# Two-block transformer kernel on one core: first attention's scores from float32r pairs, and two of the recurrence's four products per level on VectorE

## The chip, the cores and the metric

The kernel runs on one core of one Trainium2 chip. The metric is device time in microseconds (us) of one execution; lower is better. The engines are named as the profile names them: PE (TensorE matmul), PEld (TensorE weight load), DVE (VectorE), ACT (ScalarE), POOL (GpSimd), SP (the queue that issues most transfers).

## What is computed

Two transformer blocks, one behind the other, on 256 tokens (272 with 16 meta tokens in the first block) of width 2048, all in float32. What matters for this change is the first attention's scores and the gated recurrence of the second block:

```python
# differential attention, 8 heads, head size 128, queries in blocks of 128 (and the 16 meta tokens)
s1 = einsum('bhqd,bhkd->bhqk', q1, k1) * scale
s2 = einsum('bhqd,bhkd->bhqk', q2, k2) * scale
a = softmax(mask(s1)) - lam * softmax(mask(s2))

# gated recurrence, 8 heads of 128, over the tokens t
f_t = lb + (1 - lb) * sigmoid(z_t);   k_t = (1 - lb) * sigmoid(-z_t)
state_t = f_t * state_{t-1} + k_t v_t;   o_t = q_t state_t
```

## The kernel before, in words

**Weights.** All weight matrices come through one stream of 6240 tiles of 128x128, in the order in which PE uses them. `Weights.take` (lines 113 to 132) hands out a tile. A *slot* is 8 tiles. When PE's program reaches slot s, ACT is given the rounding of slot s+3 to float32r (`high`, line 84, from `raw` into `hi`), and DVE the remainder of slot s+2 (`low`, line 93, into `lo`), so that three float32r matmuls (x high by w high, x low by w high, x high by w low) stand for one of float32. `hi` has 4 buffers and `lo` has 3, so the writes for slots s+3 and s+2 go into the buffers that slot s-1 gives up.

**Ticks.** After that, once per slot, `take` calls `step_bg` (line 173). It moves the first generator of the queue `bgq` one step on, and then the first of `bgq2`; a step is what lies between two `yield`s. Heads of the first attention (`attend`) and of the second (`slide`) are in `bgq`, behind the set-up generators `first_parameters` and `rotary_tables`; the groups of the recurrence (`hgrn`) are in `bgq2`. Twice per slot `step_evac` moves the generators on that take projections out of PSUM. Every engine runs its instructions in the order in which they are written; this order is what the `yield`s set, and nothing reorders it.

**First attention, `attend` (line 785).** Its first step is empty. The second transposes v on PE (lines 792, 793) and splits it into float32r parts (`parts`, lines 766 on ACT and 767 on DVE). The third computes the scores in plain float32, six matmuls per head (lines 800 to 802): for each of the two components 144, 272 and 16 columns against 128, 128 and 16 rows. Each float32 matmul is two records of the trace. Then DVE adds the mask and takes the maxima (lines 808 to 814). q and k reach the tile `qk` from `qkv_evac`, which turns them on POOL (lines 888 to 890).

**Second attention, `slide` (line 1103).** One step has the scores (PE lines 1112, 1113) and the mask and maxima on DVE (1118 to 1125); the next has the exponentials on ACT (1128 to 1131) and, behind them, three small DVE instructions (1132 to 1134) that wait for them.

**Recurrence, `hgrn` (line 1223).** Four groups of two heads. A group works through eight levels, m = 1, 2, 4 ... 128. Per level, `products` (line 1242) issues on POOL qp (1245) and kp (1246), the operands of the level's matmuls, and for m < 128 two in-place updates, x by f (1251) and f by f (1252), for the next level. Tick lv issues `products(lv + 1)`, then the matmuls of level lv on PE (1266; 1274 for the last), then a predicated copy on DVE (1268). So the operands of level lv+1 are issued one tick before PE wants them. Groups 0 to 2 run beside the projections of the next group and one `slide` each; group 3 runs beside `gates` (1314). `hgrn_evac` (line 1188) takes the gate out of PSUM: sum, scale by the norm on DVE (1212), tanh on ACT (1214), and from it f and k by two scalings on POOL (1215, 1216).

Of the kernel before, what the change touches and what calls it, by code (L numbers as in the profile page):

```python
# [135 lines left out]
def tile_two_block_model(ctx, tc, w, xT, pT, cv_d, cs_d, msk_d, pos_d, gains, spill, aside, out):  # L136
# [27 lines left out]
    def att_t():  # L164
        return att_p.tile([P, 512], F32, tag="att", name="att")
# [224 lines left out]
    def split_pair(hi, lo, src):  # L390
        act(hi.bitcast(F32R), src)
        yield
        V.tensor_tensor(lo.bitcast(F32R), src, hi, ALU.subtract)
# [271 lines left out]
    with tc.tile_pool(name="ph0", bufs=1) as ph:  # L665
# [3 lines left out]
        for i in range(8):  # L669
            nc.sync.dma_start(h[:, 2 * i:2 * i + 2, :], xT[:, 2 * i:2 * i + 2, :])  # L670
            if i % 2 == 0 and i // 2 < RAW:
                W.load(i // 2)
        mskf = ph.tile([P, 7, 64], F32, tag="mskf", name="mskf")
        pt = ph.tile([P, 2, S], F32, tag="pt", name="pt")
        pi_t = ph.tile([P, S], I32, tag="pos", name="pos")
        x0 = Normed(h, 0, L, "pre0", tmp)
        neg_lam, sub, gnorm = prm[:, 0:1], prm[:, 1:3], prm[:, 3:4]
        fB, fA, kB, kN = prm[:, 8:16], prm[:, 16:24], prm[:, 24:32], prm[:, 32:40]
# [83 lines left out]
        def parts(n, tag, src, meta=None):  # L762

            hi, lo = meta or (ph.tile([P, n], F32, tag=tag + t, name=tag + t) for t in "hl")
            rows = NM if meta else P
            act(hi[:rows].bitcast(F32R), src)
            V.tensor_tensor(lo[:rows].bitcast(F32R), src, hi[:rows], ALU.subtract)
            return hi.bitcast(F32R), lo.bitcast(F32R)
# [16 lines left out]
        def attend(hd):  # L785
            st = heads[hd]
            qk, vf = st["qk"], st["v"]
            yield
            tv, tm = att_t(), att_t()
            for d in range(2):  # L790
                for k in range(2):
                    PE.transpose(tv[:, k * 256 + d * P:k * 256 + (d + 1) * P], vf[d][:, NM + k * P:NM + (k + 1) * P], ident)
                PE.transpose(tm[:NM, d * P:(d + 1) * P], vf[d][:, :NM], ident)
            vt, vm = parts(512, "vt", tv), parts(256, "vm", tm[:NM, :256], meta_v)
            yield
            sa, sb = att_t(), [att_t(), att_t()]
            sav = sa[:, :288].rearrange("p (c k) -> p c k", c=2)
            scv = sa[:NM, 288:320].rearrange("p (c k) -> p c k", c=2)
            for c in range(2):
                PE.matmul(sav[:, c], qk[:, c, NM:NM + P], qk[:, 2 + c, :144], start=True, stop=True)  # L800
                PE.matmul(sb[c][:, :L], qk[:, c, NM + P:], qk[:, 2 + c, :], start=True, stop=True)
                PE.matmul(scv[:, c], qk[:, c, :NM], qk[:, 2 + c, :NM], start=True, stop=True)
            ea = ph.tile([P, 2, 144], F32, tag="ea", name="ea")
            eb = ph.tile([P, 2, L], F32, tag="eb", name="eb")
            em = meta_e[:NM, :2 * NM].rearrange("p (c k) -> p c k", c=2)
# [240 lines left out]
    with tc.tile_pool(name="ph2", bufs=1) as ph:  # L1046
# [141 lines left out]
        def hgrn_evac(nt, acc):  # L1188
            kind, hd = (nt - 12) // 8, (nt - 12) % 8
            gr, i = hd // 2, hd % 2  # L1190
            st = hg.setdefault(gr, {})

            def slot(tag, bufs=1):
                if tag not in st:
                    st[tag] = hp.tile([P, 2, S], F32, tag="hg_" + tag, name=tag, bufs=bufs)
                return st[tag][:, i]

            if kind in (0, 3):
                t = tmp()
                yield from total(acc, t)  # L1200
                V.tensor_tensor(t, t, R2[0], ALU.mult)
                o = slot("q" if kind == 0 else "g")
                yield
                act(o, t, AF.Tanh, scale=0.5)
                yield
                V.scalar_tensor_tensor(o, o, 1.0, t, ALU.add, ALU.mult)
                if kind == 3 and i == 1:
                    bgq2.append(hgrn(gr))
            elif kind == 1:
                t = tmp()  # L1210
                yield from total(acc, t)
                V.tensor_tensor(t, t, R2[0], ALU.mult)
                yield
                act(t, t, AF.Tanh, scale=0.5)
                G.tensor_scalar(slot("f", 2), t, fB[:, hd:hd + 1], fA[:, hd:hd + 1], ALU.mult, ALU.add)
                G.tensor_scalar(slot("k", 2), t, kN[:, hd:hd + 1], kB[:, hd:hd + 1], ALU.mult, ALU.add)

        QP = [hp.tile([P, S], F32, tag=f"qp{i}", name=f"qp{i}") for i in range(2)]
        KP = [hp.tile([P, 2, S], F32, tag=f"kp{i}", name=f"kp{i}") for i in range(2)]
# [3 lines left out]
        def hgrn(gr):  # L1223
            st = hg[gr]
            q, k, f, vt, g = (st[n] for n in "qkfvg")
            x = mid().rearrange("p (i n) -> p i n", i=2)
            G.memset(x, 1.0)
            st_ = mid().rearrange("p (a b) -> p a b", a=4)
            s01 = mid()[:, :256].rearrange("p (a b) -> p a b", a=2)
            dg = att_t()  # L1230
            for i in range(2):
                for b in range(2):
                    c = slice(b * P, (b + 1) * P)
                    PE.matmul(dg[:, (2 * i + b) * P:(2 * i + b + 1) * P], k[:, i, c], q[:, i, c], start=True, stop=True)
            V.tensor_tensor(st_, dg.rearrange("p (a b) -> p a b", a=4), ident.unsqueeze(1).to_broadcast([P, 4, P]), ALU.mult)
            yield

            def halves(t, m):
                u = t.rearrange("p i (s e m) -> p (i s) e m", e=2, m=m)
                return u[:, :, 0, :], u[:, :, 1, :]  # L1240

            def products(lv):
                m = 1 << lv
                qp, kp = QP[lv % 2], KP[lv % 2]
                G.tensor_tensor(qp.rearrange("p (q m) -> p q m", m=m), halves(q, m)[1], halves(f, m)[1], ALU.mult)  # L1245
                G.tensor_tensor(halves(kp, m)[0], halves(k, m)[0], halves(x, m)[0], ALU.mult)  # L1246
                if m < P:
                    f0, f1 = halves(f, m)
                    x0_, _ = halves(x, m)
                    n = S // m  # L1250
                    G.tensor_tensor(x0_, x0_, f1[:, :, m - 1:m].to_broadcast([P, n, m]), ALU.mult)  # L1251
                    G.tensor_tensor(f1, f1, f0[:, :, m - 1:m].to_broadcast([P, n, m]), ALU.mult)

            products(0)
            yield
            for lv in range(8):
                if lv < 7:
                    products(lv + 1)
                qp, kp = QP[lv % 2], KP[lv % 2]
                ps = att_t()  # L1260
                if lv < 7:
                    for i in range(2):
                        for b in range(2):
                            c = slice(b * P, (b + 1) * P)
                            t = slice((2 * i + b) * 64, (2 * i + b + 1) * 64)
                            PE.matmul(ps[:, t], kp[:, i, c], qp[:, t], start=True, stop=True)
                    m = 1 << lv
                    V.copy_predicated(
                        st_.rearrange("p a (s e m) -> p (a s) e m", e=2, m=m)[:, :, 1, :],
                        msk[:, lv].rearrange("p a (s m) -> p (a s) m", m=m),  # L1270
                        ps[:, :S].rearrange("p (q m) -> p q m", m=m))
                else:
                    for i in range(2):
                        PE.matmul(ps[:, i * P:(i + 1) * P], kp[:, i, :P], qp[:, i * P:(i + 1) * P], start=True, stop=True)
                    act(s01.rearrange("p a b -> p (a b)"), ps[:, :256])
                yield
            o = att_t()
            for i in range(2):
                PE.matmul(o[:, 2 * i * P:(2 * i + 1) * P], st_[:, 2 * i], vt[:, i, 0], start=True, stop=True)
                PE.matmul(o[:, (2 * i + 1) * P:(2 * i + 2) * P], s01[:, i], vt[:, i, 0], start=True, stop=False)  # L1280
                PE.matmul(o[:, (2 * i + 1) * P:(2 * i + 2) * P], st_[:, 2 * i + 1], vt[:, i, 1], start=False, stop=True)
            sq = tiny(4, "hsq")
            for a in range(4):
                junk = tmp()
                act(junk[:, :P], o[:, a * P:(a + 1) * P], AF.Square, accum_out=sq[:, a:a + 1])
            r = rows_rsqrt(sq, 4, scale=1.0 / P)
            yield
            os_ = mid().rearrange("p (a b) -> p a b", a=4)
            V.tensor_tensor(os_, o.rearrange("p (a b) -> p a b", a=4), r.unsqueeze(2).to_broadcast([P, 4, P]), ALU.mult)
            yield  # L1290
            ot = att_t()
            for a in range(4):
                PE.transpose(ot[:, a * P:(a + 1) * P], os_[:, a], ident)
            y = mid().rearrange("p (i n) -> p i n", i=2)
            V.scalar_tensor_tensor(y, ot.rearrange("p (i n) -> p i n", i=2), gnorm, g, ALU.mult, ALU.mult)
            yield from split_pair(yh[:, 2 * gr:2 * gr + 2, 0], yh[:, 2 * gr:2 * gr + 2, 1], y)
            yield
# [281 lines left out]
```

## Time and profile before

| | |
|---|---|
| median of 3 runs | 2394.36 us (2394.22 to 2395.17) |
| the profiled execution: its own time | 2394.97 us |
| its span | 2393.2 us |
| granted clock of PE, mean | 0.997 |
| busy share of the span | PE 99%, PEld 88%, DVE 61%, ACT 49%, POOL 23% |
| chain that ended last, by engine | PE 69%, POOL 3%, DVE 1%, DMA 1% |

The profiled execution's own time is 1.8 us more than its span (what lies around the first and last instruction) and 0.6 us more than the median. A busy PE isn't PE at its peak: matmuls are pipelined and their recorded durations overlap, so the cost of one is read from the distance of its start to the start of the next. Where a line stands for several instructions ("x8"), the first number is the start of the first and the second the time to the end of the last.

### The profile page before, as it was taken

To read this page: it belongs to the slowest core of one execution; us is meant where nothing else is said; L and a number is where in the kernel's file an instruction comes from. 1 tells how busy PE (TensorE), PEld (TensorE's weight loads), DVE (VectorE), ACT (ScalarE), POOL (GpSimd) and SP (SyncE) were. 2 spreads that over 40 slices of the span, in tenths; PEclk is the share of its full clock that TensorE was granted. 3 is DMA by queue.
4 is the path that set the end of the run, shared out by engine and by line. 5 is a ranking of instruction groups with operands and counts; after the bars stand their busy time and mean duration, and the time that the engine had idled before them with its cause. 6 is when DMAs were issued, how large, how long until landed. Compare 5 with 4: busy or idle time off the path is not lost.

```text
span 2393.2 us, 36724 instructions
## 1 busy us (share of the span) xinstructions
PE 2364.7 (99%) x14560; PEld 2112.0 (88%) x14560; DVE 1468.7 (61%) x2202; ACT 1162.5 (49%) x1931; POOL 545.0 (23%) x603
## 2 busy tenths in 40 slices
PE   8999999999999999999999999999999999999998
PEld 8999999998999888898888888888888888888876
DVE  7665555547767476667656566575545555556575
ACT  5444444545555464444444454564444444344463
POOL 5433222226322003455440121011100110011000
PEclk9999999999999999999999999999999999999999
DMA  6344444544555554334345556455555555555653
GB/s 253 142 152 154 157 156 158 196 177 172 190 193 216 206 218 158 144 141 155 145 159 193 184 187 246 176 193 187 214 205 186 187 193 189 186 188 193 255 196 138
DMA packets 64875, 439.08 MB, mean 183 GB/s; under 512 B 7104, under 2 KB 10304, under 8 KB 13760
## 3 DMA queue, kind: packets, MB, share of 16 engines
q1 hardware_dynamic: 59184, 413.81, 47.5%
q0 software_dynamic: 1904, 15.34, 1.6%
q10 hardware_dynamic: 3616, 7.59, 0.9%
q8 instruction: 114, 1.87, 0.3%
q14 instruction: 57, 0.47, 0.1%
HBM read 426.75 MB, written 9.96 MB: 182 GB/s over the span
## 4 chain that ended last, share of the span: by engine, by line
PE 69%; POOL 3%; DVE 1%; DMA 1%; issue 1%; ACT 0%; DVEq 0%; ACTq 0%; POOLq 0%; SPq 0%
PE acc L215 26%; PE acc L214 13%; PE acc L247 7%; PE acc L245 7%; PE acc L246 7%; PE acc L1092 2%; PE acc L217 1%; PE acc L211 1%; PE acc L210 1%; PE acc L209 1%; DMA raw<-w 1%; POOL b L1251 1%; PE att L215 1%; POOL qp L1245 1%; POOL kp L1246 0%
## 5 line engine op out<-in xcount | busy, mean ns | idle before, releaser
L93 DVE TENSOR_TENSOR lo<-raw,hi 128x1024 fp32r<-128x1024 f32 (+1 forms) x803 | 988.5, 1235 | 635.9 <-PE acc L247 183.8
L84 ACT CAST hi<-raw 128x1024 fp32r<-128x1024 f32 x780 | 814.7, 1047 | 616.2 <-PE acc L246 208.3
L215 PE MATMUL acc<-x,hi 128*128 128x512 f32 x2656 | 929.5, 395 | 1.1 <-DVE c L274 0.6
L214 PE MATMUL acc<-x,lo 128*128 128x256 f32 x2490 | 701.4, 282 | 0.4 <-DVE lo L93 0.3
L215 PEld LDWEIGHTS acc<-x,hi 128*128 128x128 f32 x2656 | 491.7, 188 | 102.4 <-DVE x L542 1.4
L214 PEld LDWEIGHTS acc<-x,lo 128*128 128x128 f32 x2490 | 470.0, 189 | 7.6 <-DVE lo L93 0.8
L209 PE MATMUL acc<-x,hi 128*128 128x272 f32 (+3 forms) x1232 | 358.9, 291 | 7.3 <-ACT hi L84 7.2
L211 PE MATMUL acc<-x,lo 128*128 128x272 f32 (+3 forms) x1232 | 355.8, 289 | 0.5 <-DVE lo L93 0.4
L210 PE MATMUL acc<-x,hi 128*128 128x272 f32 (+3 forms) x1232 | 355.2, 288 | 0.8 <-DVE x L426 0.8
L209 PEld LDWEIGHTS acc<-x,hi 128*128 128x128 f32 x1232 | 232.8, 189 | 8.4 <-ACT hi L84 7.2
L210 PEld LDWEIGHTS acc<-x,hi 128*128 128x128 f32 x1232 | 234.7, 191 | 2.0 <-DVE x L426 1.3
L211 PEld LDWEIGHTS acc<-x,lo 128*128 128x128 f32 x1232 | 232.5, 189 | 1.0 <-DVE lo L93 1.0
L168 ACT ACTIVATE c<-acc 128x256 f32<-128x256 f32 x210 | 80.1, 384 | 257.0 <-PE acc L215 254.8
L1381 POOL TENSOR_TENSOR c<-c,R 128x256 f32<-128x256 f32 x88 | 66.7, 759 | 579.0 <-DVE c L274 576.9
L247 PE MATMUL acc<-lo,up 128*128 128x512 f32 x352 | 138.7, 394 | 0.3 <-DVE lo L93 0.3
L245 PE MATMUL acc<-hi,up 128*128 128x512 f32 x352 | 138.8, 394 | 0.0
L246 PE MATMUL acc<-hi,up 128*128 128x512 f32 x352 | 138.4, 393 | 0.0
L274 DVE TENSOR_TENSOR c<-c,acc 128x256 f32<-128x256 f32 x206 | 84.8, 413 | 11.3 <-ACT c L168 11.3
L215 PE MATMUL acc<-yy,hi 128*128 128x512 f32 x256 | 87.6, 396 | 0.0
L247 PEld LDWEIGHTS acc<-lo,up 128*128 128x128 f32 x352 | 66.1, 188 | 16.0 <-DVE lo L93 0.7
L246 PEld LDWEIGHTS acc<-hi,up 128*128 128x128 f32 x352 | 66.3, 188 | 15.3
L245 PEld LDWEIGHTS acc<-hi,up 128*128 128x128 f32 x352 | 66.1, 188 | 15.1
(381 smaller groups left out, 3377.9 us busy)
## 6 DMA issues: line engine op xcount, KB each, us to landing
raw<-w SPq DMA_DIRECT2D x389, 1024.0 KB, 4.8
h<-spill POOLq DMA_DIRECT2D x2, 2048.0 KB, 10.4
spill<-h POOLq DMA_DIRECT2D x2, 2048.0 KB, 9.2
h<-xT SPq DMA_DIRECT2D x8, 272.0 KB, 9.3
yx<-xT POOLq DMA_DIRECT2D x1, 2176.0 KB, 14.8
spill<-ht ACTq DMA_DIRECT2D x8, 256.0 KB, 5.8
y<-gains ACTq DMA_DIRECT2D x2, 1024.0 KB, 6.0
he<-spill POOLq DMA_DIRECT2D x1, 2048.0 KB, 10.9
```

Source lines behind the costliest of these rows:

```text
L84: self.nc.scalar.copy(hi.bitcast(F32R), self.part(s))
L93: self.nc.vector.tensor_tensor(lo[:, c].bitcast(F32R), self.part(s)[:, c], hi[:, c], ALU.subtract)
L168: A.activation(out, in_, func, **kw)
L209: PE.matmul(acc[:, :n], whi, x[:, 0], start=first, stop=False)
L210: PE.matmul(acc[:, :n], whi, x[:, 1], start=False, stop=False)
L211: PE.matmul(acc[:, :n], wlo, x[:, 0], start=False, stop=last)
L214: PE.matmul(acc[:, S:], wlo, x[:, 0], start=False, stop=False)
L215: PE.matmul(acc.rearrange("p (t n) -> p t n", t=2), whi, x, start=first, stop=last)
L245: PE.matmul(acc, xh, whi, start=i == 0, stop=False)
L246: PE.matmul(acc, xl, whi, start=False, stop=False)
L247: PE.matmul(acc, xh, wlo, start=False, stop=i == len(kts) - 1)
L274: V.tensor_tensor(dst, dst, acc[:, :S], ALU.add)
```

## The change

1. In `attend`, the first step now rounds the whole of `qk` (128x1088) to float32r on ACT (`qkh`), and the second step has DVE take the remainder (`qkl`), ahead of the split of v. The scores are three float32r matmuls each (high by high, low by high, high by low) in place of one of float32: 18 per head in place of 6.
2. In `hgrn_evac`, f and k come from two ACT instructions in place of two on POOL.
3. In `hgrn`, the two in-place updates of a level move from POOL to DVE, out of `products` into a function `updates`, which tick lv issues ahead of `products(lv + 1)`. Before, `products(lv)` ended with them one tick earlier.
4. Three start-up tiles of the first phase share buffers with tiles of `attend` that are first written later, which makes room for `qkh` and `qkl`.

```diff
-        mskf = ph.tile([P, 7, 64], F32, tag="mskf", name="mskf")
-        pt = ph.tile([P, 2, S], F32, tag="pt", name="pt")
-        pi_t = ph.tile([P, S], I32, tag="pos", name="pos")
+        mskf = ph.tile([P, 2, L], F32, tag="eb", name="mskf")...
+        pt = ph.tile([P, 2, S], F32, tag="os", name="pt")
+        pi_t = ph.tile([P, 2, 144], F32, tag="ea", name="pos")...
...
             qk, vf = st["qk"], st["v"]
+            qkh, qkl = (ph.tile([P, 4, L], F32, tag="qk" + t, name="qk" + t) for t in "hl")
+            split = split_pair(qkh, qkl, qk)
+            next(split)
             yield
...
+            next(split, None)
             vt, vm = parts(512, "vt", tv), parts(256, "vm", tm[:NM, :256], meta_v)
             yield
+            qr = [t.bitcast(F32R) for t in (qkh, qkl)]
+
+            def score(out, c, a, n):
+                for i, j in ((0, 0), (1, 0), (0, 1)):
+                    PE.matmul(out, qr[i][:, c, a], qr[j][:, 2 + c, :n], start=i + j == 0, stop=j == 1)
...
             for c in range(2):
-                PE.matmul(sav[:, c], qk[:, c, NM:NM + P], qk[:, 2 + c, :144], start=True, stop=True)
-                PE.matmul(sb[c][:, :L], qk[:, c, NM + P:], qk[:, 2 + c, :], start=True, stop=True)
-                PE.matmul(scv[:, c], qk[:, c, :NM], qk[:, 2 + c, :NM], start=True, stop=True)
+                score(sav[:, c], c, slice(NM, NM + P), 144)
+                score(sb[c][:, :L], c, slice(NM + P, L), L)
+                score(scv[:, c], c, slice(0, NM), NM)
...
-                G.tensor_scalar(slot("f", 2), t, fB[:, hd:hd + 1], fA[:, hd:hd + 1], ALU.mult, ALU.add)
-                G.tensor_scalar(slot("k", 2), t, kN[:, hd:hd + 1], kB[:, hd:hd + 1], ALU.mult, ALU.add)
+                act(slot("f", 2), t, AF.Identity, scale=fB[:, hd:hd + 1], bias=fA[:, hd:hd + 1])
+                act(slot("k", 2), t, AF.Identity, scale=kN[:, hd:hd + 1], bias=kB[:, hd:hd + 1])
...
-                if m < P:
-                    f0, f1 = halves(f, m)
-                    x0_, _ = halves(x, m)
-                    n = S // m
-                    G.tensor_tensor(x0_, x0_, f1[:, :, m - 1:m].to_broadcast([P, n, m]), ALU.mult)
-                    G.tensor_tensor(f1, f1, f0[:, :, m - 1:m].to_broadcast([P, n, m]), ALU.mult)
+            def updates(lv):
+                m = 1 << lv
+                f0, f1 = halves(f, m)
+                x0_, _ = halves(x, m)
+                n = S // m
+                V.tensor_tensor(x0_, x0_, f1[:, :, m - 1:m].to_broadcast([P, n, m]), ALU.mult)
+                V.tensor_tensor(f1, f1, f0[:, :, m - 1:m].to_broadcast([P, n, m]), ALU.mult)
...
                 if lv < 7:
+                    updates(lv)
                     products(lv + 1)
```

## Rows read from the trace of the kernel before

**Rows 1.** The page: TensorE's busy time, share of the span and instructions.

```profile
PE 2364.7 (99%) x14560; PEld 2112.0 (88%) x14560; DVE 1468.7 (61%) x2202; ACT 1162.5 (49%) x1931; POOL 545.0 (23%) x603
```

**Rows 2.** Timeline of PE, the last head's scores: start, us, engine, line, form, count.

```profile
413.87 0.41 PE L800 MATMUL att<-qk 128*128 128x144 f32 x2
414.11 0.62 PE L801 MATMUL att<-qk 128*128 128x272 f32 x2
414.66 0.21 PE L802 MATMUL att<-qk 128*16 128x16 f32 x2
...
415.85 0.39 PE L209 MATMUL acc<-x,hi 128*128 128x272 f32 x1
416.08 0.29 PE L210 MATMUL acc<-x,hi 128*128 128x272 f32 x1
416.21 0.29 PE L211 MATMUL acc<-x,lo 128*128 128x272 f32 x1
```

**Rows 3.** Timeline of PE at the recurrence's first level.

```profile
967.14 1.00 PE L1266 MATMUL att<-qp,kp 128*128 128x64 f32 x8
967.95 0.48 PE L215 MATMUL acc<-x,hi 128*128 128x512 f32 x1
```

**Rows 4.** Timelines of PE and of DVE at the first head's scores.

```profile
69.17 0.41 PE L800 MATMUL att<-qk 128*128 128x144 f32 x2
...
68.80 1.20 DVE L93 TENSOR_TENSOR lo<-raw,hi 128x1024 fp32r<-128x1024 f32 x1
69.93 0.67 DVE L767 TENSOR_TENSOR vtl<-att,vth 128x512 fp32r<-128x512 f32 x1
```

**Rows 5.** Timeline of DVE, the last head: v's split, ahead of its scores.

```profile
411.85 0.69 DVE L767 TENSOR_TENSOR vtl<-att,vth 128x512 fp32r<-128x512 f32 x1 [0.17 <-ACT vth L168]
```

**Rows 6.** Line 1266: what PE and PEld waited for before it (us, times).

```profile
  POOL kp L1246: 8.1, 15
```

**Rows 7.** Timeline of PE, group 3: levels 0 and 1, and the last.

```profile
1184.94 1.00 PE L1266 MATMUL att<-qp,kp 128*128 128x64 f32 x8
1188.62 1.00 PE L1266 MATMUL att<-qp,kp 128*128 128x64 f32 x8
...
1213.68 0.71 PE L1274 MATMUL att<-qp,kp 128*128 128x128 f32 x4
```

**Rows 8.** Timeline of POOL, group 3: the two products of a level.

```profile
1199.86 0.75 POOL L1245 TENSOR_TENSOR qp<-q,f 128x256 f32<-128x256 f32 x1
1200.57 0.73 POOL L1246 TENSOR_TENSOR kp<-k,b 128x256 f32<-128x256 f32 x1
```

**Rows 9.** Timeline of DVE, group 3 (one tick) and group 0 (level 1).

```profile
1201.32 1.23 DVE L93 TENSOR_TENSOR lo<-raw,hi 128x1024 fp32r<-128x1024 f32 x1 [2.85 <-ACT hi L84]
...
1202.84 0.41 DVE L274 TENSOR_TENSOR c<-c,acc 128x256 f32<-128x256 f32 x1
...
972.42 0.73 DVE L1268 COPY_PREDICATED b<-msk,att 128x256 f32<-128x256 uint8 x1
```

**Rows 10.** Timeline of PE, group 0: levels 4, 5 and 6.

```profile
982.82 1.10 PE L1266 MATMUL att<-qp,kp 128*128 128x64 f32 x8
...
986.61 1.00 PE L1266 MATMUL att<-qp,kp 128*128 128x64 f32 x8
...
990.84 1.10 PE L1266 MATMUL att<-qp,kp 128*128 128x64 f32 x8 [0.40 <-POOL kp L1246]
```

**Rows 11.** Timeline of DVE, group 0: level 4's copy, then the slide's waits for ACT.

```profile
985.18 0.43 DVE L1268 COPY_PREDICATED b<-msk,att 128x256 f32<-128x256 uint8 x1
...
990.14 0.66 DVE L1132 TENSOR_TENSOR sm<-sm,es 128x4 f32<-128x4 f32 x1 [1.72 <-ACT es L168]
...
991.05 0.46 DVE L1134 TENSOR_SCALAR sm<-sm 128x4 f32<-128x4 f32 x1
```

**Rows 12.** Timeline of ACT, group 0: tanh of the gate, then a cast of weights.

```profile
986.89 0.42 ACT L168 ACTIVATE c<-c 128x256 f32<-128x256 f32 x1 [3.51 <-DVE c L1212]
987.21 1.04 ACT L84 CAST hi<-raw 128x1024 fp32r<-128x1024 f32 x1
```

More of the change, by code (lines that the diff above doesn't have):

```diff
@@ L672, in tile_two_block_model @@
                 W.load(i // 2)
-        mskf = ph.tile([P, 7, 64], F32, tag="mskf", name="mskf")
-        pt = ph.tile([P, 2, S], F32, tag="pt", name="pt")
-        pi_t = ph.tile([P, S], I32, tag="pos", name="pos")
+        mskf = ph.tile([P, 2, L], F32, tag="eb", name="mskf").rearrange("p a b -> p (a b)")[:, :448].rearrange("p (l m) -> p l m", l=7)
+        pt = ph.tile([P, 2, S], F32, tag="os", name="pt")
+        pi_t = ph.tile([P, 2, 144], F32, tag="ea", name="pos").rearrange("p a b -> p (a b)")[:, :S].bitcast(I32)
         x0 = Normed(h, 0, L, "pre0", tmp)
```

## The prediction, made before the changed kernel ran

> **What bounds the kernel now.** I read the page first: PE is busy for 2364.7 of 2393.2 us [rows 1]. No other engine comes near, so work taken from PE, or a wait of PE, moves the end one for one, and work on DVE, ACT or POOL costs nothing until PE waits for it. So I went to the timeline of PE at the two changed places, to what line 1266 waits for, and last to DVE, ACT and POOL at those moments, to see what each has in its queue ahead of the moved work.
>
> In the first attention PE waits for nothing: weights of 272 columns go by at 0.13 us each and the scores stand between them [rows 2]. In the recurrence PE does wait, for POOL's kp, 8.1 us over both of its queues [rows 6]. PE's own loss is read from the ticks. A tick without a wait is 1188.62 - 1184.94 = 3.68 us, and group 3's seven take 1213.68 - 1184.94 = 28.74 [rows 7], so 28.74 - 25.76 = 2.98 are lost there. In group 0 two ticks take 990.84 - 982.82 = 8.02 in place of 7.36 [rows 10]: 0.66. Groups 1 and 2 repeat it. All that POOL costs PE is thus some 3.0 + 3 x 0.66 = 5.0 us.
>
> **The change, part by part.**
>
> *Scores.* The six float32 matmuls of a head take 415.85 - 413.87 = 1.98 us, and the first weight matmul behind them 0.23 where others take 0.13: 2.08 in all. 144 columns cost 0.24 and 272 cost 0.55, which leaves 0.20 of a component's 0.99 for 16 [rows 2]. Of the new 18, those of 272 columns have a row of their own kind: 0.13. No row shows float32r under 256 columns. The nearest by width is line 1266, whose eight records of 64 columns, each with 128 columns of weights, take 967.95 - 967.14 = 0.81 [rows 3]: 0.10 each although little streams, so the weight load sets a floor. I take 0.12 for 144 columns, between floor and 0.13, and 0.08 for 16 (only 16 columns of weights, float32 took 0.20 for two records). A head: 2 x 3 x (0.12 + 0.13 + 0.08) = 1.98, which saves 0.10, or **0.8 us** over eight heads. Three passes for one gain hardly anything where weights set the pace. Lower end, if only columns count (0.07 and 0.01): 1.26 a head, a saving of 6.6. Upper end, if each narrow one costs what float32 does (0.24 and 0.20): 3.42 a head, a loss of 10.7.
>
> *The split of q and k.* Rounding 1088 elements is a cast like that of 1024 (1.04 on ACT [rows 12]), in a step that was empty; ACT is half idle [rows 1]. The remainder is 1.13 x 1088/1024 = 1.20 on DVE (by the 1.13 from line 93 to its successor [rows 4]), right ahead of v's split. In the last head v's split starts at 411.85, after waiting for ACT, and the scores at 413.87 [rows 2, 5]: 2.0 of room for 1.2, so nothing. Without that cover it would cost up to 2.3 a head. In the first head the cover is gone: DVE is behind with the rotary tables, v's split starts at 69.93, when the scores have been running since 69.17 [rows 4]. There PE would wait until 69.93 + 1.20 = 71.13: **+2.0 us**, and PE queues the weight matmuls behind that wait. Bounds 0 (DVE takes it in an idle moment) and 3 (ACT late too).
>
> *f and k on ACT.* Two instructions of 0.3 (the distance from tanh to its successor [rows 12]) stand right behind the tanh, ahead of what ACT does next. They take 0.6 out of whatever follows; they are priced with the slide below.
>
> *The updates on DVE.* POOL's level shrinks to its two products, 0.71 + 0.73 = 1.44 [rows 8], so POOL alone would never be late. But the chain now crosses engines inside one tick: DVE's line 93 first (it can't start before PE ends the slot, so at the tick's start), 1.13 [rows 4]; then two updates, 0.41 each by the nearest 128x256 product on DVE [rows 9]; then 1.44 on POOL; then PE. That is 3.39 plus hand-offs of 0.2 as an estimate: 3.6 against the 3.68 of a tick. It fits by a hair. For m = 1 and 2 DVE may be slower on strided operands: line 1268 took 0.73 at level 1 against 0.43 at level 4 [rows 9, 11], which would add up to 0.5 a level. I take 0.1 for each of the two levels. Group 3: -2.98 + 0.2 = -2.8.
>
> *The slide in front of them.* `bgq` steps ahead of `bgq2`, so in groups 0 to 2 the updates stand behind the slide's DVE work, which POOL never had to wait for. In the score tick (level 4) DVE gets to its copy at 985.18 [rows 11]; updates and products would end at 985.18 + 0.82 + 1.44 + 0.2 = 987.6, where PE wants them at 982.82 + 3.68 = 986.5: 1.1 late. In the next tick DVE sits in line 1132 waiting for the exponentials until 990.14 and is through at 991.51 [rows 11]; ACT is 0.6 later by f and k; then 0.82 + 1.44 + 0.2 give 994.6 for level 6, which PE started at 990.84 [rows 10]. That is 3.7 later; part of the slide's slowness was POOL working beside it (0.66 for a 128x4 instruction), work that is gone. I take **3.0** for the two ticks, bounds 2.3 and 3.7. What waits behind PE's stopped matmul is the whole weight stream. Recurrence: 3 x (3.0 + 0.2) - 2.8 = **+6.8**; bounds 3 x 2.3 - 3.0 = +3.9 and 3 x 4.7 - 2.0 = +12.1.
>
> *Shared start-up buffers*: `attend` first writes them behind the first head's scores, 69.17 [rows 4]; the start-up work that reads them stands far ahead of that in every engine's order. Nothing, and no more than the wait already priced for that head if one were late.
>
> Sum: -0.8 + 2.0 + 6.8 = **+8.0 us**. The profiled execution's own time is 2394.97, 0.6 over the median of 2394.36. On its time the sum gives 2403.0, on the median **2402.4**.
>
> **The rivals.** (A difference of 0.2%, 4.8 us, is about what a measurement of this kernel can tell from none.)
>
> *Narrow float32r at float32's rate.* If 144 columns take 0.24 each, a head takes 2 x 3 x (0.24 + 0.13 + 0.08) = 2.70, +0.62, or +5.0 in all; with the rest +13.8: 2408.2. It would mean that the change doesn't save passes at all where it says so. For it: every 32-bit record here under 256 columns runs slower than a column per 0.13/272 us [rows 2, 3]. Against it: those are of float32.
>
> *Three passes for four.* If passes alone count, the block falls to three quarters: 2.08 x 0.25 x 8 = 4.2 saved; with the rest +4.6: 2399.0. Against it: the floor of 0.10 per weight load [rows 3]. The Trainium skill has this rule (FP8 and Floating Point Precision, TensorE Precision Notes): true float32 takes four passes through the array, which would make three float32r matmuls three quarters of it. The float32 rows agree, 0.24 for 144 columns [rows 2]; for narrow float32r no row here shows it.
>
> *The updates hide, not slower.* DVE idles 2.85 us in one tick of group 3 [rows 9]. If DVE is done with both updates within 3.68 - 1.44 = 2.24 us of each tick's start, also beside the slide, PE never waits and the 5.0 us come back: -5.0 + 2.0 - 0.8 = -3.8, 2390.6. That point decides; the slide's ticks speak against it, by 2.5 us and more [rows 11]. The Trainium skill points this way (GPSIMD Engine Reference, Engine selection): elementwise work belongs on VectorE, about twice as fast. The rows agree on the speed, 0.41 against POOL's 0.73 [rows 8, 9]; which queue is waited for the rule doesn't ask.
>
> **How the numbers follow.** The forecast gets 0.38 (2398 to 2407 by its bounds), narrow at float32's rate 0.28, three passes 0.15, hidden updates 0.19. Slower by over 0.2% (above 2399.2): 0.34 of the first, the second whole, 0.06 of the third, 0.02 of the last, where the narrow matmuls are dear too: 0.70. Faster by over 0.2% (below 2389.6) needs hidden updates and cheap scores: 0.10. Same: 0.20. The range, 2394 to 2412, takes in the second case and the upper bound of the recurrence, and leaves out most of the hidden case and the ends of the dearest scores.
>
> **What would show it.** Right: a wait of PE for the new remainder of some 2 us near 69 us and at no other head; scores of about 2.0 us a head; line 1266 waiting for kp in two ticks of groups 0 to 2 by 1 and 2 to 3 us, and hardly in group 3. Wrong: score blocks of 1.5 or 2.7 us; no waits for kp beside the slide; ticks of group 3 that stay over 4 us, which would mean that the chain through DVE is longer than read; or PE waiting for weights (line 84 or 93) in either stage because ACT or DVE got too much.

## The result and the profile after

The changed kernel takes 2417.01 us (median of 3 runs, 2416.90 to 2418.84) where the kernel before takes 2394.36: a ratio of 1.0096, 95% interval 1.0083 to 1.0109. It is slower by 22.7 us; forecast were 8.0 us more, and 2417 lies outside the range. The profiled execution took 2417.01 us with a span of 2414.6, 21.4 longer than before.

The page's engine line, to compare with [rows 1]:

```profile
PE 2371.5 (98%) x14608; PEld 2121.3 (88%) x14608; DVE 1490.3 (62%) x2266; ACT 1179.0 (49%) x1955; POOL 475.5 (20%) x531
```

PE is busy for 6.8 us more and idle for 14.6 more (2414.6 - 2371.5 against 2393.2 - 2364.7). POOL lost 70 us of work, and still the kernel got slower.

**The first attention.** Timeline of PE, the last head's scores [rows 2]:

```profile
412.21 0.23 PE L804 MATMUL att<-qkh 128*128 128x144 f32 x1
412.28 0.28 PE L804 MATMUL att<-qkh,qkl 128*128 128x144 f32 x1
412.39 0.27 PE L804 MATMUL att<-qkl,qkh 128*128 128x144 f32 x1
412.50 0.33 PE L804 MATMUL att<-qkh 128*128 128x272 f32 x1
...
412.92 0.17 PE L804 MATMUL att<-qkh 128*16 128x16 f32 x1
412.95 0.17 PE L804 MATMUL att<-qkh,qkl 128*16 128x16 f32 x1
...
413.88 0.37 PE L209 MATMUL acc<-x,hi 128*128 128x272 f32 x1
414.09 0.29 PE L210 MATMUL acc<-x,hi 128*128 128x272 f32 x1
```

The pitch is read from start to start: 0.11 us for 144 columns, 0.03 for 16. To the second weight matmul behind the scores a head takes 414.09 - 412.21 = 1.88 where it took 416.08 - 413.87 = 2.21: 0.33 less. Heads 1 to 6 give the same, so it is some 2.6 over eight heads. Timelines of PE and then of DVE at head 0 [rows 4]:

```profile
68.07 0.23 PE L804 MATMUL att<-qkh 128*128 128x144 f32 x1
70.20 0.34 PE L804 MATMUL att<-qkh,qkl 128*128 128x144 f32 x1 [1.90 <-DVE qkl L393]
...
68.87 1.27 DVE L393 TENSOR_TENSOR qkl<-qk,qkh 128x1088 fp32r<-128x1088 f32 x1
70.08 0.67 DVE L767 TENSOR_TENSOR vtl<-att,vth 128x512 fp32r<-128x512 f32 x1
```

PE waits 1.90 us for the remainder here, and at no other head.

**The recurrence.** The list of PE's waits gives what PE alone, without its weight loads, waited for at the recurrence's matmuls (us, times, the longest). Before, it was 2.7 us in 7 waits. Now it is:

```profile
PE att L1279 <- POOL kp L1256: 14.2, 6, 3.7
```

The seven ticks of a group are read from each level's first matmul to the next level's, in us (the fourth tick ends where level 4 starts, the sixth where level 6 does):

| group | before | after |
|---|---|---|
| 0 | 3.68 3.69 3.68 4.63 3.79 4.23 4.45 = 28.15 | 3.96 3.79 3.87 5.94 3.76 7.51 7.10 = 35.93 |
| 1 | 3.68 3.69 3.68 4.63 3.79 4.23 4.45 = 28.15 | 3.97 3.79 3.87 5.86 3.78 7.50 6.01 = 34.78 |
| 2 | 3.68 3.69 3.68 4.63 3.79 4.35 4.41 = 28.23 | 3.97 3.79 3.87 5.86 3.78 7.49 7.56 = 36.32 |
| 3 | 3.68 4.12 4.16 4.45 4.00 4.39 3.94 = 28.74 | 3.87 4.07 3.78 3.85 3.75 3.95 3.80 = 27.07 |

The sums grow by 134.10 - 113.27 = 20.8 us, nearly all of the loss: +1.7 in the first three ticks of groups 0 to 2, +3.8 in their fourth, where the slide's rotary products run on POOL, -0.1 in the fifth, +9.7 in the sixth, +7.4 in the seventh, and -1.7 in group 3. Timelines of PE in group 0 [rows 10] and in group 3 [rows 7]:

```profile
984.59 1.10 PE L1279 MATMUL att<-qp,kp 128*128 128x64 f32 x8 [1.13 <-POOL kp L1256]
988.35 1.00 PE L1279 MATMUL att<-qp,kp 128*128 128x64 f32 x8
995.86 1.97 PE L1279 MATMUL att<-qp,kp 128*128 128x64 f32 x8 [3.67 <-POOL kp L1256]
...
998.59 0.63 PE L215 MATMUL acc<-x,hi 128*128 128x512 f32 x1
1002.96 0.61 PE L1287 MATMUL att<-qp,kp 128*128 128x128 f32 x4
...
1207.14 1.00 PE L1279 MATMUL att<-qp,kp 128*128 128x64 f32 x8
...
1234.21 0.61 PE L1287 MATMUL att<-qp,kp 128*128 128x128 f32 x4
```

PE stands still for 3.67 us. After it the same work costs more: the eight matmuls of a level take 1.97 instead of 1.00, one of line 215 takes 0.63 instead of 0.39. The activity by windows of 3 us says why. Its columns are the window, its length, the busy time of PE, PEld, DVE, ACT and POOL with the number of instructions, the granted clock, the DMA share and GB/s:

```profile
993.00:996.00 3.00, 0.14 (x1) 0.14 (x1) 2.38 (x4) 0.55 (x1) 2.39 (x2) 0.80 0.25 104
996.00:999.00 3.00, 3.00 (x12) 2.83 (x13) 1.79 (x5) 0.00 (x0) 1.41 (x2) 0.50 0.00 0
999.00:1002.00 3.00, 3.00 (x12) 2.55 (x11) 0.08 (x1) 1.51 (x3) 0.00 (x0) 0.56 0.01 3
```

The granted clock falls from 1.00 to 0.50, that is from 2.4 to 1.2 GHz, behind the wait, and is back at 1.00 from 1002 on. The timelines of ACT [rows 12], DVE [rows 11] and POOL [rows 8] at that moment show what PE waited for:

```profile
988.96 1.03 ACT L84 CAST hi<-raw 128x1024 fp32r<-128x1024 f32 x1
989.90 0.40 ACT L168 ACTIVATE e<-e,nb 128x128 f32<-128x128 f32 x1
...
991.67 0.19 ACT L168 ACTIVATE es<-es 128x4 f32<-128x4 f32 x1
...
991.89 0.16 DVE L1142 TENSOR_TENSOR sm<-sm,es 128x4 f32<-128x4 f32 x1 [2.27 <-ACT es L168]
...
992.38 0.42 DVE L1263 TENSOR_TENSOR b<-b,f 128x256 f32<-128x256 f32 x1
992.83 0.42 DVE L1264 TENSOR_TENSOR f<-f 128x256 f32<-128x256 f32 x1
...
993.50 1.73 DVE L93 TENSOR_TENSOR lo<-raw,hi 128x1024 fp32r<-128x1024 f32 x1
...
993.42 0.72 POOL L1255 TENSOR_TENSOR qp<-q,f 128x256 f32<-128x256 f32 x1 [5.35 <-DVE f L1264]
994.10 1.71 POOL L1256 TENSOR_TENSOR kp<-k,b 128x256 f32<-128x256 f32 x1
```

Read backwards: PE waits for kp; POOL had idled 5.35 us for the update of f; that update stood in DVE's queue behind line 1142, which sat 2.27 us until ACT had done the slide's exponentials; and ACT did f, k and a cast of weights first. Last, kp takes 1.71 instead of the 0.73 of [rows 8], and line 93 on DVE runs beside it.

At the fourth tick another queue is in the way. Timeline of POOL, group 0, the first of the slide's three rotary products and the operands of level 4 behind them:

```profile
978.64 1.78 POOL L1081 TENSOR_TENSOR c<-c,rope 128x256 f32<-128x256 f32 x1
...
982.13 0.74 POOL L1255 TENSOR_TENSOR qp<-q,f 128x256 f32<-128x256 f32 x1
982.82 1.72 POOL L1256 TENSOR_TENSOR kp<-k,b 128x256 f32<-128x256 f32 x1
```

Before, the rotary products began at 977.50 and kp was done at 982.00. Now POOL first waits 2.28 us for DVE's update with the operands of level 3, which stand ahead of the rotary products, and kp meets line 93 here too (1.72). It ends at 984.54, and PE starts level 4 at 984.59.

### The profile page after: what moved, and what is told of

It is laid out like the page before. It is cut to its first block, busy times and chain, and to the rows that moved or that the text cites. A ratio compares the mean times of both kernels' runs of the same rounds, so it can differ in the third digit from the quotient of the medians.

```text
span 2414.6 us, 36821 instructions
## 1 busy us (share of the span) xinstructions
PE 2371.5 (98%) x14608; PEld 2121.3 (88%) x14608; DVE 1490.3 (62%) x2266; ACT 1179.0 (49%) x1955; POOL 475.5 (20%) x531
## 3 DMA queue, kind: packets, MB, share of 16 engines
q8 instruction: 115, 1.88, 0.3%
## 4 chain that ended last, share of the span: by engine, by line
PE 71%; DVE 2%; POOL 1%; ACT 1%; issue 0%; DMA 0%; DVEq 0%; ACTq 0%; POOLq 0%
PE acc L215 27%; PE acc L214 13%; PE acc L246 7%; PE acc L247 7%; PE acc L245 7%; PE acc L1102 2%; PE acc L217 1%; PE acc L210 1%; PE acc L211 1%; PE acc L209 1%; PE att L1279 1%; PE att L215 1%; DVE lo L93 0%; DMA raw<-w 0%; PE att L524 0%
## 5 line engine op out<-in xcount | busy, mean ns | idle before, releaser
L168 ACT ACTIVATE c<-c 128x256 f32<-128x256 f32 (+1 forms) x84 | 35.3, 420 | 94.0 <-POOL c L1394 39.3
L245 PEld LDWEIGHTS acc<-hi,up 128*128 128x128 f32 x352 | 66.4, 189 | 15.9
```

Of the source, the lines that this page charges most:

```text
L168: A.activation(out, in_, func, **kw)
L245: PE.matmul(acc, xh, whi, start=i == 0, stop=False)
```

## The experiments

The theory after this is that the recurrence carries the loss, through (a) updates that queue on DVE behind a wait for ACT, (b) the rotary products ahead of qp and kp on POOL, (c) the clock after a stop. For every run below the text gives the median, its ratio to the kernel before, timed on the same chip (2394.15 to 2394.95), and the 95% interval of the ratio.

**Halves of the change.** First: the scores alone, the recurrence as before.

> The changed kernel with the recurrence and f and k as before: parts 1 and 4 of the change alone. Theory (the recurrence carries the whole loss): the scores save 0.33 a head, 2.6 us, and the first head's wait for qkl gives 1.9 back, so 2393 to 2394.5, next to no difference from before. Rival (the scores with their split cost ACT and DVE time that PE later waits for): 2398 or more.

Second: the recurrence alone, the scores as before.

> The kernel before with only f and k on ACT and the two updates on DVE: parts 2 and 3 alone. Theory (the ticks of the four groups sum to +20.8 between first and last level, whatever the scores do): 2414 to 2417. Rival (part of the loss comes from both parts together, as ACT and DVE fill up): under 2410.

The scores alone take 2396.38 us, ratio 1.0008 (0.9999 to 1.0017), which lies between the theory and its rival. The recurrence alone takes 2416.89, 1.0092 (1.0077 to 1.0107), as the theory said, with group sums of 36.09, 34.79, 36.38 and 27.25. So the recurrence carries the loss.

The scores' expected small gain did not come. In the profile of the scores alone PE is 1.9 us ahead of the kernel before when it leaves the last head's scores, and it loses that at two later places. The first is at 588 us. PE waits there for the same in both kernels (1.42 and 0.68 us at line 350), but the granted clock falls earlier, so that 1.2 us are lost. The windows of 4 us, of the kernel before and then of the scores alone:

```profile
588.00:592.00 4.00, 1.66 (x12) 1.49 (x12) 3.04 (x6) 1.32 (x2) 1.26 (x3) 1.00 0.84 297
588.00:592.00 4.00, 2.74 (x13) 2.48 (x13) 1.67 (x5) 0.00 (x0) 0.86 (x1) 0.59 0.74 231
```

The second is at 902 us. PE gets to line 1102's first matmul 0.9 us earlier than in the kernel before, but leaves the wait behind it no earlier. Timelines of PE and of ACT in the run of the scores alone:

```profile
898.69 0.28 PE L1102 MATMUL acc<-hi,x 128*128 128x256 f32 x1
902.12 0.39 PE L1102 MATMUL acc<-lo,x 128*128 128x256 f32 x1 [3.15 <-DVE lo L93]
...
894.16 1.05 ACT L84 CAST hi<-raw 128x1024 fp32r<-128x1024 f32 x1 [5.54 <-DMA raw<-w]
```

And of the same place (line 1092 for PE) in the kernel before:

```profile
899.57 0.28 PE L1092 MATMUL acc<-hi,x 128*128 128x256 f32 x1
901.85 0.39 PE L1092 MATMUL acc<-lo,x 128*128 128x256 f32 x1 [2.00 <-DVE lo L93]
...
893.87 1.05 ACT L84 CAST hi<-raw 128x1024 fp32r<-128x1024 f32 x1 [4.34 <-DMA raw<-w]
```

The wait grows from 2.00 to 3.15, since line 93 stands on DVE behind rotary work that did not come earlier. That work waits for a result of ACT (line 168), which stands behind the cast of line 84, and the cast waits for a weight transfer that lands at 894.16 instead of 893.87. What is left of the scores' gain is waited away there; why the transfer lands no earlier is left open.

**f and k back on POOL**, the rest of the change kept:

```
-act(slot("f", 2), t, AF.Identity, ...)
+G.tensor_scalar(slot("f", 2), t, ...)
...
```

> The changed kernel with f and k back on POOL. Theory (ACT's two instructions, 1.0 us, stand ahead of the slide's exponentials, and DVE, the updates, POOL and PE follow them): level 6's wait of 3.7 falls to about 2.7 in groups 0 to 2, 3 us in all; and if it is the length of that wait that takes PE's clock to its lower level, the clock stays up behind it too, 7 us more: 2407. Rival (the clock falls behind any wait there): 2414. Rival (f and k cost nothing): 2417.

It takes 2414.64, 1.0082 (1.0065 to 1.0099), as the first rival said. The sixth tick is 7.17 instead of 7.50. Of the 1.2 us that f and k are recorded with on ACT only 0.33 come back, as the exponentials then wait for the cast of line 84, and that waits for PE. PE's wait is still 3.3 us and the clock falls behind it.

**PE kept busy in the wait**: 30 dummy matmuls ahead of level 6 in groups 0 to 2.

```
+if lv == 6 and gr < 3:
+    for _ in range(30):
+        PE.matmul(ps[:, S:], xs2(0)[:, 0, :P], xs2(0)[:, 0], start=True, stop=True)
```

> The changed kernel with 30 float32r matmuls of 256 columns (0.12 each, 3.5 us), whose results nobody reads, ahead of level 6's matmuls in groups 0 to 2, so that PE works where it waited 3.7 us. Theory (the ticks behind that wait are long because PE's clock falls in it): the granted clock stays at 1.00, the tick behind it falls from 7.1, 6.0 and 7.6 us to 4.5, and 7 us go: 2410. Rival (they are long because DVE and ACT are behind): 2417 or more.

It takes 2410.90, 1.0068 (1.0053 to 1.0083), as the theory said. The sixth tick stays at 7.5. The seventh falls from 7.10, 6.01 and 7.56 to 4.46, 4.45 and 4.47, together 7.3 us, which is what it was before the change, and the windows of that stretch show full clock:

```profile
993.00:996.00 3.00, 2.91 (x25) 2.71 (x24) 2.37 (x4) 0.65 (x1) 2.41 (x2) 1.00 0.29 123
996.00:999.00 3.00, 3.00 (x20) 2.78 (x21) 2.36 (x5) 0.26 (x1) 1.43 (x2) 1.00 0.02 5
999.00:1002.00 3.00, 3.00 (x22) 2.70 (x22) 1.23 (x1) 2.97 (x7) 0.00 (x0) 1.00 0.01 3
```

This shows that the clock costs 6 to 7 us on top of the waits.

**The recurrence stepped ahead of the slide**, so that its updates stand ahead of line 1142:

```
-for q in (bgq, bgq2):
+for q in (bgq2, bgq):
```

> The changed kernel with the two queues stepped the other way round, so that a tick's updates stand ahead of the slide's work on DVE and not behind it. Theory (the waits at levels 4 and 6 come from standing behind the slide, whose last instructions wait for the exponentials; the chain line 93, updates, products alone takes about a tick): levels 4, 6 and 7 fall to some 4.8, 4.0 and 4.8 us, the clock stays up, groups 0 to 2 take 29 to 29.5 us in place of 34.8 to 36.3: 2396 to 2400. Rival (the crossing from DVE to POOL is too slow by itself): over 2408.

It takes 2410.19, 1.0069 (1.0055 to 1.0083), which is the rival's time. The long sixth tick is gone (3.71), but the fourth is still 5.9, with a stop of PE of 1.9 us: the rotary products hold POOL until 1058.29, ahead of qp and kp, so it is not the crossing by itself, as the rival had it. Timelines of POOL and PE, group 1:

```profile
1058.94 1.71 POOL L1256 TENSOR_TENSOR kp<-k,b 128x256 f32<-128x256 f32 x1
...
1060.70 1.10 PE L1279 MATMUL att<-qp,kp 128*128 128x64 f32 x8 [1.91 <-POOL kp L1256]
```

The clock falls behind this wait of 1.91 too (windows of 3 us from 1062 on read 0.65 and 0.78).

**The updates a tick earlier**, right behind the products whose operands they overwrite; then the same with the remainder of q and k a step earlier; then the same without the new scores. The edit of the first:

```
 products(0)
+updates(0)
...
-updates(lv)
 products(lv + 1)
+if lv < 6:
+    updates(lv + 1)
```

> The changed kernel with the updates of a level issued on DVE right behind that level's products, one tick earlier, in the order in which POOL had them. Theory (DVE is fast enough; only the tick in which it is asked is too late): a whole tick of slack, no wait of PE for kp, groups 0 to 2 at 27.4 us and group 3 at 26: 5 us under the kernel before in the recurrence, in all 2389 to 2392. Rival (DVE, blocked on POOL's products, delays line 93 and the slide instead): 2396 or more.

> As the run with the updates a tick earlier, and DVE's remainder of q and k moved from attend's second step into its first, behind ACT's rounding. Theory (the first head's wait of 1.9 us is DVE's place in the order): it falls to about 0.5, 1.4 us less than the run with the updates earlier alone: 2387.5 to 2391. Rival (DVE waits for the rounding and holds line 93 up at every head): slower than that run by 1 us or more.

> The kernel before with only f and k on ACT and the updates on DVE a tick earlier; scores in float32 as before. Theory (the float32r scores are worth 2.6 less 1.9 us): within 1 us of the run with the updates a tick earlier, 2389 to 2392. Rival (the scores' part costs time somewhere that the stages do not show): 2 us or more faster than that run.

The first takes 2407.87, 1.0057 (1.0044 to 1.0071), far over its theory and in the rival's range. With the remainder of q and k a step earlier it is 2408.16, 1.0055 (1.0042 to 1.0067), neither faster nor slower by 1 us. With the old scores it is 2406.29, 1.0053 (1.0040 to 1.0066), 1.6 faster than the first, between theory and rival; the three intervals overlap. The first three ticks are at 3.68 again and the sixth too, but the updates of level 6 are still behind line 1142, and the wait moves to the last level, in a tick of 7.3. So it is the slide's wait for ACT again that holds them, and not POOL's products, as the rival had it. Timelines of DVE and PE in the first, group 0:

```profile
998.22 0.16 DVE L1142 TENSOR_TENSOR sm<-sm,es 128x4 f32<-128x4 f32 x1 [2.73 <-ACT es L168]
...
999.16 0.43 DVE L1264 TENSOR_TENSOR f<-f 128x256 f32<-128x256 f32 x1
...
1002.20 0.71 PE L1289 MATMUL att<-qp,kp 128*128 128x128 f32 x4 [2.80 <-POOL kp L1256]
```

**Both cures together** (the recurrence stepped first and the updates a tick earlier), then with the remainder earlier as well, and that remainder alone on the scores-alone kernel:

> The change, with the level updates issued a tick earlier AND the recurrence stepped ahead of the sliding attention, so that the updates stand ahead of the softmax sums (L1142) in VectorE's queue and have a whole tick of slack. Theory (the remaining 13 us of the two single cures come from updates that still stand behind L1142, which waits for the exps on ScalarE, and from the clock that falls in the PE wait that follows): the tick of 7.3 us (levels 6 to 7) goes to 3.7 to 4.5, only the rotary tick stays at about 5.1, a group takes 27 to 28.2 us (28.15 to 28.74 before), no PE wait over 1 us at the recurrence's matmuls and no half-clock spell in the groups: 2391 to 2397 us. Rival (VectorE is blocked at updates that wait for GpSimd's products, and the sliding attention and the weight remainders behind them come late instead): group sums stay over 29.5 us and the time at 2402 or more.

> The run before (updates a tick earlier, recurrence stepped first) with the remainder of the first attention's scores subtracted one step earlier. Theory: the PE wait of head 0 goes from 1.9 us to about 1.2 (it then also waits for the value remainder, L767), and the spell at half clock that now and then follows it goes: 0.5 to 2 us under the run before, 2390 to 2396 us. Rival (the wait of head 0 has no weight in the end, since the phase's work after it is paced by something else): within 0.3 us of the run before.

> The scores alone (recurrence as before), with the remainder subtracted one step earlier. The scores' blocks take 0.33 us less in each of 8 heads (2.6 us) and the wait of head 0 is 1.2 in place of 1.9 us. Theory (these are PE time on the path, so they add up): 2392 to 2394.5 us, under the scores alone (2396.4) by 1 to 3 us. Rival (what the scores gain is lost again behind them, at evictions that set the pace in that phase): 2395 to 2397 us.

With both cures it takes 2403.13, 1.0036 (1.0023 to 1.0050). The ticks behind line 1142 are at 3.68, as the theory said, but the time is the rival's and so are the sums of two groups (28.36, 29.85 and 29.85 in groups 0 to 2). What is left lies at the rotary products. Timelines of POOL, DVE and PE, group 0:

```profile
981.58 1.56 POOL L1081 TENSOR_TENSOR c<-c,rope 128x256 f32<-128x256 f32 x1 [3.63 <-DVE c L1080]
...
985.29 0.73 POOL L1256 TENSOR_TENSOR kp<-k,b 128x256 f32<-128x256 f32 x1
...
986.05 0.42 DVE L1263 TENSOR_TENSOR b<-b,f 128x256 f32<-128x256 f32 x1 [3.51 <-POOL kp L1256]
...
986.07 1.11 PE L1281 MATMUL att<-qp,kp 128*128 128x64 f32 x8 [1.29 <-POOL kp L1256]
```

Three rotary products hold POOL from 981.58 to 984.6, qp and kp come behind them, and PE and DVE wait. In groups 1 and 2 the clock falls behind this wait. With the remainder earlier it takes 2401.20, 1.0032 (1.0020 to 1.0043). Its gain of 1.9 is not told from none, as the intervals overlap; PE's wait at head 0 fell to 0.4 + 0.8, the second part for v's remainder (line 767). On the scores alone the same edit gives 2394.86, 1.0001 (0.9993 to 1.0010), just between its theory and its rival. So whether the scores gain anything in the end is not settled, only that it is less than these runs can tell.

**The slide's rotary products on DVE too:**

```
-G.tensor_tensor(sh, sh, sin2, ALU.mult)
-(G if v_done else V).tensor_tensor(t, t, cos2, ALU.mult)
-G.tensor_tensor(t, t, sh, ALU.add)
+R = V if v_done else G
+R.tensor_tensor(sh, sh, sin2, ALU.mult)
+V.tensor_tensor(t, t, cos2, ALU.mult)
+R.tensor_tensor(t, t, sh, ALU.add)
```

> The run before (updates a tick earlier, recurrence first, remainder earlier) with the sliding attention's rotary products (L1081 to L1083) on VectorE too. Theory (what is left of the loss, 2401.2 against 2394.2, comes from the rotary products on GpSimd, 3.0 us that stand ahead of qp and kp, so that PE waits 1.3 and 0.5 us there and the clock falls to its lower level behind it): the waits at the recurrence's matmuls go from 5.3 to under 2 us, no half-clock spell is left in the groups, each group takes 26.5 to 28 us, and the time comes 6 to 10 us under that run: 2391 to 2395 us. Rival (VectorE, with remainders, rotary, softmax and updates, is now the engine that PE waits for): PE waits for VectorE's results in the groups instead, 2398 us or more.

It takes 2393.90, 0.9996 (0.9987 to 1.0005), 7.3 us under the run before it (on another chip), as the theory said. No window in the groups is under full clock, and the groups' ticks sum to 26.79 three times and 27.94. This is all that PE waits for between 960 and 1225:

```profile
PE att L1282 <- POOL kp L1257: 1.4, 3, 0.6
```

From the first level of group 0 to the last of group 3 it takes 1213.39 - 969.25 = 244.1 us against 1213.68 - 967.14 = 246.5: 2.4 less than before. (Within a group the sum understates the work, as the slide's transposes, 0.8 us, now follow the last level.) In the whole kernel that gain can't be told from none: this version ties with the kernel before, and no version tried beats it.

## Why the prediction was wrong

The sign was right, and so was one of the two places of the wait: level 6, behind the slide. The recurrence's size was not: +6.8 forecast, +20.8 in the ticks, 14.0 short. The sum failed most at two terms that it didn't have: what a stop of PE costs after it (7.4 of the 14.0) and POOL's rotary products ahead of qp and kp (3.8). The small levels and group 3 lack 1.1 each, the slide's tick 0.7. Step by step:

- **No term for the clock** is the step that failed. The prediction says that the whole weight stream waits behind PE's stopped matmul and prices the stop at its own length. But the seventh tick, in which PE hardly waits, adds 7.4 us: each stop cost 1.6 to 3.2 us more behind it, at half clock, and the dummy matmuls gave that back. The kernel before shows such a fall itself, behind the wait of 2.00 us at line 1092:

```profile
902.00:905.00 3.00, 3.00 (x17) 3.00 (x18) 2.96 (x4) 2.30 (x4) 2.86 (x3) 0.61 0.00 0
```

- **No term for the rotary products.** At the fourth tick qp and kp stand behind three rotary products on POOL, 1.3 us a group. The prediction looked at what stands ahead of the moved work on DVE, and not at what it makes late on POOL. The 1.1 that it expected at level 5 instead did not come: the fifth tick is 3.76 to 3.78, where it was 3.79.
- **The slide in front of the updates.** Its own working had level 6 3.7 us later (994.6 against 990.84 [rows 10]), both ticks together. I took 3.0, because "part of the slide's slowness was POOL working beside it", work that would be gone. The sixth tick adds 3.2, so the size is about right, though in one tick and not in two; PE starts level 6 5.0 later (995.86), with the fourth tick and the small levels in it. DVE's small instructions did get quick (line 1142 takes 0.16; as line 1132 it took 0.66 [rows 11]), but now it is kp that meets line 93: it takes 1.71 for 0.73. qp, line 93 and kp go from 993.42 to 995.81, 2.39 us; one behind the other they would take 0.72 + 1.13 (line 93 to its successor [rows 4]) + 0.73 = 2.58, and qp and kp alone 1.4. The Trainium skill has this (SBUF — State Buffer, Who interferes with whom): a VectorE instruction with two inputs from SBUF contends with a GpSimd instruction that reads it. These rows agree. Before the change such a meeting could fall on an update instead, for which PE did not wait. Timeline of POOL, group 0, beside line 93 from 981.90 on, in the kernel before:

```profile
982.08 1.55 POOL L1251 TENSOR_TENSOR b<-b,f 128x256 f32<-128x256 f32 x1
```

- **f and k on ACT**: 0.6 taken, 0.33 measured by the run that moves them back.
- **The small levels**: 0.2 a group taken, 0.57 measured. The chain was read as 3.6 us in a tick of 3.68; at the first level it takes 3.76, from line 93's start at 967.17 to kp's end at 970.93: the updates are not slower there, as was feared (0.42), but qp and kp are (0.86 and 0.85). A tick earlier it fits, 3.68 each. Of its parts the hand-offs, an estimate of 0.2, were about right: 0.17 from DVE's f to POOL's qp and 0.05 from kp to PE at level 6. **Group 3**: -2.8 taken, -1.7 measured. Its ticks end at 3.75 to 4.07, not at 3.68, and PE's weight loads still wait 1.5 us for kp there.
- **Scores**: their blocks saved 2.6 in place of 0.8. The 144 columns cost 0.11 (0.12 taken), the 16 columns 0.03 (0.08 taken). The Trainium skill would have given the short ones (TensorE: Matmul & The Clock Gate, Wait — 56ns, not 53.3ns?): matmuls start no closer than about 25 ns, however few the columns. The rows agree with it. The rival of three passes for four had the right sign, but at 4.2 it was too large; none of the rivals counted that the gain is lost again at 588 and 902 us.
- **Head 0's wait**: 2.0 taken, 1.9 measured. **No cost at the other heads**: right, no other wait at line 804.
- **The rival of hidden updates** named the right point (updates done in time, beside the slide too), and the last experiment nearly reaches it. Of the 5.0 us read from the ticks 2.4 come back: 0.5 in each of groups 0 to 2, 0.8 in group 3. Most of the rest is still waiting, since the last version's ticks in group 3 hold 2.2 us over 7 x 3.68 and PE's weight loads wait 2.3 us for kp there.

## What to carry to other kernels

Before taking work from a side engine, read what the bounding engine loses to it: here some 5 us of 2393 by the ticks, of which the best version won back 2.4. That is little against the new waits that the move can make. Then read the queue that the work is moved into: whatever stands ahead and waits (here a softmax sum for exponentials) makes the moved work late, and it helps to issue it earlier and ahead of that. Read the queue of the next engine of the chain too (here the rotary products on POOL). Price a stop of TensorE with the slower matmuls that can follow it.

## What was not expected of the hardware

- The granted clock fell behind waits of 3.67, but also of 1.91 and of 1.28 us, and not always. In the run with both cures the wait at the rotary tick is 1.29, 1.28 and 1.29 us in groups 0, 1 and 2; full clock follows it in group 0, windows of 0.68 to 0.75 in the other two. Longer waits passed without a fall as well: 1.96 us in group 0 of the run with the recurrence stepped first, and 2.97 us in group 1 of the run with the updates a tick earlier. So the length of a wait alone doesn't decide it; what does is left open.
- In four of the versions' profiles (f and k on POOL, updates a tick earlier, both cures, rotary products on DVE) the clock also fell for some us after head 0's scores, in the others it did not. In these four the recurrence starts at 969.3 to 971.3 us, in the others at 966.5 to 967.7: a single execution moves by 2 to 4 us, which is likely part of why edits of 1 or 2 us could not be told apart.
